# Wider passes for a mixer's natural-order projections, and attention values computed the other way round

## The chip, the cores and the metric

The kernel runs on one core of a Trainium2 chip. The time is the device time of one execution in microseconds; the kernel before takes 1060.43 us, the median of three runs (1059.81 to 1061.07). The engines of the core work side by side, each through its own list of instructions in a fixed order: TensorE (PE) multiplies matrices, VectorE (DVE) and ScalarE (ACT) do elementwise work, GpSimd (POOL) some of it and part of the DMA issues, and SyncE (SP) issues most DMAs.

## The reference

One decoder layer over 1024 tokens of width 1024. With RMS norms around each part it computes

```
p = rmsnorm(x) @ W_in      # columns split into q_a, k_a, v_a, q_r, k_r, v_r, g
a = sliding-window attention(q_a, k_a, v_a)    # 8 heads, 2 groups of keys and values, window 128, sinks
r = swish(g) * groupnorm(retention(q_r, k_r, v_r))   # 4 heads of 128, chunks of 128, rotated q and k
x = x + rmsnorm(concat(a, r) @ W_out)
u = causal conv3(rmsnorm(x) @ W_up);  x = x + rmsnorm((gelu(u_gate) * u_val) @ W_down)
```

The first projection has six groups of columns: attention queries (512), keys (128), values (128), retention queries and keys (512 each), retention values (512) and gates (512). Only the first projection, and the order of the work around it, is touched.

## The kernel before, in words

All products are in float32, made of three products of rounded halves: an operand is split into a rounded part `h` and a rest `l`, and `mm3` (lines 127 to 131) adds h\*h, h\*l and l\*h into one PSUM tile. Weights come by SP's DMA queue into a ring of three buffers (`load_w`), and are split by `split` into a ring of five pairs: the rounded part by ACT (line 119), the rest by DVE (line 120).

The 1024 tokens are worked in two halves `hh` of 512. There are two ways to project a half. `block` (line 133) makes a transposed result, 128 columns of the weight on the partitions and 512 tokens along the row: 8 steps of 3 matmuls of 512 columns into one large PSUM tile. It serves attention queries (`q_unit`, 4 blocks), keys (`k_unit`) and retention queries and keys (`rot_unit`, 8 blocks). `nat_unit` (line 262) makes a natural result, 128 tokens on the partitions and weight columns along the row: the tokens of a half are four blocks `b`, each with its own large PSUM tile, and a pass `w` covers 384 weight columns in four units `kk` of two steps each, so 24 matmuls of 384 columns per unit. Three passes cover 1152 columns: pass 0 the attention values and half of the retention values, pass 1 the other half and 128 columns of the gates, pass 2 the other 384 gate columns. After unit 3 of a pass the four tiles are emptied: attention values are scaled by the row norm and split (ACT line 282, DVE line 283), retention values copied (lines 289 and 293), gates turned into `(tanh(g r / 2) + 1) g` (ACT line 299, DVE line 300).

PSUM has four large tiles (`big`) and four small ones (`small`) in rings. A pass needs all four large ones; a `block` needs one.

What stands next to what is written out by hand. A half has a first list of units (queries, the sums for the norm `half_sums`, which have no matmul, `setup`, keys, pass 0) and a second one (8 rotation units, passes 1 and 2). `interleave` (line 504) puts steps of a second list behind each unit, spread evenly: in the first list of half 1 the retention of half 0, in the second list of each half its own attention. Attention (`att_stages`) has 8 items of scores, flip and output; the flip of an item is listed two items after its scores, the output one after the flip, 24 stages in all. Retention (`ret_stages`) has per chunk an inner step (products and transposes of the keys), an output step and a flip, 12 in all. The output step multiplies the masked inner product, which DVE writes (line 407), by the values.

A planner then fixes each engine's list from that order: it goes through the program with estimated durations and gives an engine the earliest instruction that it takes to be ready. Each engine keeps that list on the chip and waits by semaphores. The order in time of PE in the profile is the order of the program, up to one place in the later up-projection.

The functions that the change touches:

Of the kernel before, what the change touches and what calls it, by code (L numbers as in the profile page):

```python
# [8 lines left out]
F32 = mybir.dt.float32  # L9
# [5 lines left out]
P = 128  # L15
# [12 lines left out]
def tile_hymba_layer(  # L28
# [94 lines left out]
    def split_w(src, n, step, name):  # L123
        raw = load_w(src, n, name)
        return [split(raw[:, c : c + step], f"{name}_{c}", step) for c in range(0, n, step)]
# [131 lines left out]
    def turns(kk):  # L257
        if kk in (0, 3):
            return [(b, i) for b in range(4) for i in range(2)]
        return [(b, i) for i in range(2) for b in range(4)]  # L260

    def nat_unit(hh, w, kk, act, st):
        if kk == 0:
            st["pn"] = [big(f"pn{hh}_{w}_{b}") for b in range(4)]
        ops = split_w(w_inN[w, kk], 768, 384, f"n{hh}_{w}_{kk}")
        ah, al = act
        for b, i in turns(kk):
            k = 2 * kk + i
            hi, lo = ops[i]
            bs = slice(b * P, b * P + P)  # L270
            lh = ah[k // 4][:, k % 4, bs]
            ll = al[k // 4][:, k % 4, bs]
            mm3(st["pn"][b][:, :384], lh, ll, hi[:, :384], lo[:, :384], k == 0, k == 7)
        if kk < 3:
            return
        _, r, _, rhf, _, _ = st["cols"]
        for b in range(4):
            ps = st["pn"][b]
            if w == 0:
                va = m.tile([P, 2, P], F32R, tag="va", name=f"va{hh}_{b}", bufs=5)  # L280
                pv = ps[:, 0:P].rearrange("p (g d) -> p g d", g=2)
                nc.scalar.activation(va[:, :, 0:64], pv, AF.Copy, scale=r[:, b : b + 1])
                nc.vector.scalar_tensor_tensor(
                    out=va[:, :, 64:128], in0=pv, scalar=r[:, b : b + 1], in1=va[:, :, 0:64].bitcast(F32),
                    op0=ALU.mult, op1=ALU.subtract,
                )
                st["va"][4 * hh + b] = va
                vr = m.tile([P, H], F32, tag="vr", name=f"vr{hh}_{b}", bufs=4)
                nc.scalar.activation(vr[:, 0:256], ps[:, 128:384], AF.Copy)
                st["vr"][b] = vr  # L290
            else:
                if w == 1:
                    nc.scalar.activation(st["vr"][b][:, 256:512], ps[:, 0:256], AF.Copy)
                    st["gp"][b] = m.tile([P, H], F32, tag="gp", name=f"gp{hh}_{b}", bufs=4)
                src = ps[:, 256:384] if w == 1 else ps[:, 0:384]
                dst = st["gp"][b][:, 0:128] if w == 1 else st["gp"][b][:, 128:512]
                n = 128 if w == 1 else 384
                th = ttile(f"th{hh}_{w}_{b}")
                nc.scalar.activation(th[:, :n], src, AF.Tanh, scale=rhf[:, b : b + 1])
                nc.vector.scalar_tensor_tensor(  # L300
                    out=dst, in0=th[:, :n], scalar=1.0, in1=src, op0=ALU.add, op1=ALU.mult
                )

# [214 lines left out]
    for hh in range(2):  # L518
# [21 lines left out]
        first += [(q_unit, hh, 2, act, st), (half_sums, hh, st, (2, 3)), (q_unit, hh, 3, act, st), (setup,)]  # L540
        first += [(k_unit, hh, act, st)]
        first += [(nat_unit, hh, 0, kk, act, st) for kk in range(4)]
        interleave(first, prev)
        second = [(rot_unit, hh, t, h, act, st) for t in range(2) for h in range(4)]
        second += [(nat_unit, hh, w, kk, act, st) for w in (1, 2) for kk in range(4)]
        interleave(second, att_stages(hh, st), 0.95)
# [683 lines left out]
```

## Time and profile before

| | before |
|---|---|
| median of the runs | 1060.43 us (1059.81 to 1061.07) |
| profiled execution | 1060.02 us, of which the span is 1058.3 us |
| granted TensorE clock | 0.998 |
| PE busy | 1046.2 us (99%) |
| DVE busy | 819.2 us (77%) |
| ACT busy | 590.7 us (56%) |
| POOL busy | 115.9 us (11%) |
| first projection, retention and attention | from 0 to about 304 us of the span |

The times of the profile are from the first to the last instruction, so the profiled execution's own time is 1.7 us longer than its span. A row in order of time gives start, duration, engine, line, what is written and read, and, in brackets, how long the engine was idle before and who released it. Matmuls overlap: a row's duration is longer than the distance to the next row's start.

### The profile page before, as it was taken

Reading aid. Unit: us, or ns where it says so; the run is one execution under the profiler, and the core shown is the slowest. Engines: PE = TensorE matmul, PEld = TensorE weight load, DVE = VectorE, ACT = ScalarE, POOL = GpSimd, SP = SyncE. Lnnn points to the kernel's source line nnn. Section 1 sums busy time; section 2 is a strip of 40 time slices with the busy share of each in tenths; the row PEclk is TensorE's granted clock in tenths of the full one; section 3 lists DMA queues with packets and bytes.
Section 4 is the critical chain, followed back from the end, with each engine's and each line's share of the span. In section 5 each row is a group of like instructions: output and inputs, shape, how many; then the busy total and the mean of one; then the engine's idle time right before and its main releaser. Section 6 shows DMA issues by size and latency. Waiting matters only on the chain.

```text
span 1058.3 us, 14252 instructions
## 1 busy us (share of the span) xinstructions
PE 1046.2 (99%) x5000; PEld 887.3 (84%) x5000; DVE 819.2 (77%) x1409; ACT 590.7 (56%) x1138; POOL 115.9 (11%) x140
## 2 busy tenths in 40 slices
PE   9999999999999999999999999999999999999996
PEld 7988998988998888888888888888888888888885
DVE  5567777667686686987797888977878898859695
ACT  7566772466662567665555455555555546445461
POOL 1013232124322110000000000000000000000033
PEclk9999999999999999999999999999999999999999
DMA  8422543221231473854323233233233695604576
GB/s 309 133 80 61 179 174 56 94 81 61 65 107 53 166 252 116 292 212 147 139 88 121 94 116 139 95 114 119 91 139 109 240 350 167 225 35 167 179 195 116
DMA packets 54152, 150.20 MB, mean 142 GB/s; under 512 B 6464, under 2 KB 6592, under 8 KB 54080
## 3 DMA queue, kind: packets, MB, share of 16 engines
q1 hardware_dynamic: 51840, 145.09, 40.7%
q0 software_dynamic: 1952, 3.68, 2.2%
q8 instruction: 39, 0.64, 0.2%
q10 hardware_dynamic: 288, 0.52, 0.1%
q14 instruction: 33, 0.27, 0.1%
HBM read 123.57 MB, written 25.69 MB: 141 GB/s over the span
## 4 chain that ended last, share of the span: by engine, by line
issue 58%; PE 35%; ACT 2%; DVE 2%; POOL 2%; DMA 1%; SPq 0%; DVEq 0%; POOLq 0%; ACTq 0%
PE pn L128 3%; PE pn L130 3%; PE pn L129 3%; PE ps_r L128 3%; PE ps_r L129 3%; PE ps_r L130 3%; PE po L130 2%; PE po L128 2%; PE po L129 2%; DMA wr_n<-w_inN 1%; PE ps_q L129 1%; PE ps_q L130 1%; PE ps_q L128 1%; PE pS L329 1%; PE pS L328 1%
## 5 line engine op out<-in xcount | busy, mean ns | idle before, releaser
L128 PE MATMUL pd<-oh_d,sh_d 128*128 128x512 f32 x264 | 103.8, 393 | 0.0
L129 PE MATMUL pd<-ol_d,sh_d 128*128 128x512 f32 x264 | 103.2, 391 | 0.0
L130 PE MATMUL pd<-oh_d,sl_d 128*128 128x512 f32 x264 | 103.0, 390 | 0.0
L1023 POOL TENSOR_TENSOR fs<-fs,mhalf 128x1 f32<-128x1 f32 x8 | 8.8, 1105 | 593.8 <-DVE fs L1020 593.8
L720 DVE SCALAR_TENSOR_TENSOR a<-uv,cvp,a 128x1023 f32<-128x1023 f32 (+1 forms) x44 | 56.2, 1278 | 21.1 <-ACT a L717 21.1
L128 PE MATMUL pn<-oh_n,xh 128*128 128x384 f32 x192 | 65.7, 342 | 0.2 <-DVE q L235 0.2
L130 PE MATMUL pn<-oh_n,xl 128*128 128x384 f32 x192 | 64.5, 336 | 0.0
L129 PE MATMUL pn<-ol_n,xh 128*128 128x384 f32 x192 | 64.2, 335 | 0.0
L130 PEld LDWEIGHTS pd<-oh_d,sl_d 128*128 128x128 f32 x264 | 49.6, 188 | 11.3
L128 PEld LDWEIGHTS pd<-oh_d,sh_d 128*128 128x128 f32 x264 | 49.6, 188 | 10.7
L129 PEld LDWEIGHTS pd<-ol_d,sh_d 128*128 128x128 f32 x264 | 49.6, 188 | 10.5
L720 DVE SCALAR_TENSOR_TENSOR a<-ug,cvp,a 128x1023 f32<-128x1023 f32 (+1 forms) x44 | 56.2, 1278 | 1.6 <-ACT a L717 1.6
L128 PE MATMUL ps_r<-xh,oh_r 128*128 128x512 f32 x128 | 50.6, 395 | 0.0
L130 PE MATMUL ps_r<-xh,ol_r 128*128 128x512 f32 x128 | 50.0, 391 | 0.0
L129 PE MATMUL ps_r<-xl,oh_r 128*128 128x512 f32 x128 | 49.9, 390 | 0.0
L346 ACT ACTIVATE s<-s,sc,r 128x128 f32<-128x128 f32 x64 | 30.9, 483 | 30.2 <-DVE sc L340 30.2
L119 ACT ACTIVATE oh_n<-wr_n 128x384 fp32r<-128x384 f32 x48 | 24.1, 521 | 32.3 <-PE ps_q L129 8.5
L119 ACT ACTIVATE oh_o<-wr_o 128x512 fp32r<-128x512 f32 x32 | 20.0, 634 | 33.7 <-PE po L130 33.6
L728 ACT ACTIVATE sh_d<-r 128x512 fp32r<-128x512 f32 x33 | 20.8, 629 | 30.5 <-PE pd L129 23.7
L754 DVE TENSOR_TENSOR raw<-raw 128x512 f32<-128x512 f32 x22 | 15.2, 689 | 29.2 <-DMA raw<-w_u 29.1
L717 ACT ACTIVATE a<-ug,cvp 128x1024 f32<-128x1024 f32 x22 | 27.3, 1240 | 18.4 <-DVE ug L882 15.3
L128 PEld LDWEIGHTS pn<-oh_n,xh 128*128 128x128 f32 x192 | 36.1, 188 | 1.0 <-issue 0.5
(1248 smaller groups left out, 3274.4 us busy)
## 6 DMA issues: line engine op xcount, KB each, us to landing
raw<-w_u SPq DMA_DIRECT2D x44, 512.0 KB, 4.4
yd<-a SPq DMA_DIRECT2D x22, 512.0 KB, 2.9
r<-yd SPq DMA_DIRECT2D x22, 512.0 KB, 5.2
wr_n<-w_inN SPq DMA_DIRECT2D x24, 384.0 KB, 3.3
wr_r<-w_inT SPq DMA_DIRECT2D x16, 512.0 KB, 3.4
wr_o<-w_o SPq DMA_DIRECT2D x16, 512.0 KB, 3.6
wr_e<-w_u SPq DMA_DIRECT2D x11, 512.0 KB, 4.1
ud<-e SPq DMA_DIRECT2D x11, 512.0 KB, 4.5
```

What stands on the lines that cost most here:

```text
L119: in_turn("oh", nc.scalar.activation(hi[:, :n], src, AF.Copy))
L128: ins = nc.tensor.matmul(ps, lh, rh, start=first, stop=False, skip_group_check=onto)
L129: nc.tensor.matmul(ps, lh, rl, start=False, stop=False, skip_group_check=onto)
L130: nc.tensor.matmul(ps, ll, rh, start=False, stop=end, skip_group_check=onto)
L328: nc.tensor.matmul(ps[:, i, :nk], lq, kkh[:, gi, k0 : k0 + nk], start=True, stop=False)
L329: nc.tensor.matmul(ps[:, i, :nk], lq, kkl[:, gi, k0 : k0 + nk], start=False, stop=True)
L346: nc.scalar.activation(s[:, i, :], s[:, i, :], AF.Exp, scale=r8, bias=c[:, 1, i : i + 1], accum_out=c[:, 3, i : i + 1])
L717: nc.scalar.activation(a, u[:, c0 : c0 + n], AF.Identity, scale=cvp[:, b, 2:3], bias=cvp[:, b, 3:4])
L720: nc.vector.scalar_tensor_tensor(out=a[:, s:], in0=u[:, c0 + s - d : c0 + n - d], scalar=cvp[:, b, tap : tap + 1], in1=a[:, s:], op0=ALU.m ...
L728: in_turn("sh", nc.scalar.activation(hi, src, AF.Copy))
L754: nc.vector.tensor_tensor(out=a11, in0=a11, in1=a21, op=ALU.subtract)
L1023: nc.gpsimd.tensor_tensor(out=ss[:, 2:3], in0=ss[:, 3:4], in1=mhalf[:, 0:1], op=ALU.pow)
```

## The change

The weight of the natural passes is now the 1024 columns of retention values and gates, in two passes of 512 columns, so that pass 0 is all retention values and pass 1 all gates. A unit has 24 matmuls of 512 columns. The attention values leave the natural passes. A new `v_unit` makes them with `block`, transposed, as one more block of 128 weight columns; ACT copies the PSUM tile to SBUF, PE turns its four 128x128 parts back into one small PSUM tile, and ACT and DVE scale and split them as before.

The order changes with it. `v_unit` stands behind `k_unit` in the first list of both halves. In half 0 the retention values move from the end of the first list to the second, behind the 8 rotation units and ahead of the gates, so the second list still has 16 units. In half 1 they stay at the end of the first list, which has 13 units in place of 12; the second list has 12 in place of 16.

```diff
+    def v_unit(hh, act, st):
+        ps = block(w_inT[13], act, f"v{hh}")
+        vt = ttile(f"vt{hh}")
+        nc.scalar.activation(vt, ps, AF.Copy)
+        pt = small(f"pvt{hh}")
+        for b in range(4):
+            nc.tensor.transpose(pt[:, b * P : b * P + P], vt[:, b * P : b * P + P], ident)
+        r = st["cols"][1]
+        for b in range(4):
+            va = m.tile([P, 2, P], F32R, tag="va", name=f"va{hh}_{b}", bufs=5)
+            pv = pt[:, b * P : b * P + P].rearrange("p (g d) -> p g d", g=2)
+            nc.scalar.activation(va[:, :, 0:64], pv, AF.Copy, scale=r[:, b : b + 1])
+            nc.vector.scalar_tensor_tensor(
+                out=va[:, :, 64:128], in0=pv, scalar=r[:, b : b + 1], in1=va[:, :, 0:64].bitcast(F32),
+                op0=ALU.mult, op1=ALU.subtract,
+            )
+            st["va"][4 * hh + b] = va
...
-        ops = split_w(w_inN[w, kk], 768, 384, f"n{hh}_{w}_{kk}")
+        ops = split_w(w_inN[w, kk], 1024, H, f"n{hh}_{w}_{kk}")
...
-            mm3(st["pn"][b][:, :384], lh, ll, hi[:, :384], lo[:, :384], k == 0, k == 7)
+            mm3(st["pn"][b], lh, ll, hi, lo, k == 0, k == 7)
...
-                nc.scalar.activation(vr[:, 0:256], ps[:, 128:384], AF.Copy)
+                nc.scalar.activation(vr, ps, AF.Copy)
...
+                gp = m.tile([P, H], F32, tag="gp", name=f"gp{hh}_{b}", bufs=4)
+                th = ttile(f"th{hh}_{b}")
+                nc.scalar.activation(th, ps, AF.Tanh, scale=rhf[:, b : b + 1])
+                nc.vector.scalar_tensor_tensor(out=gp, in0=th, scalar=1.0, in1=ps, op0=ALU.add, op1=ALU.mult)
...
-        first += [(k_unit, hh, act, st)]
-        first += [(nat_unit, hh, 0, kk, act, st) for kk in range(4)]
+        first += [(k_unit, hh, act, st), (v_unit, hh, act, st)]
+        values = [(nat_unit, hh, 0, kk, act, st) for kk in range(4)]
+        second = [(rot_unit, hh, t, h, act, st) for t in range(2) for h in range(4)]
+        if hh == 0:
+            second += values
+        else:
+            first += values
         interleave(first, prev)
-        second = [(rot_unit, hh, t, h, act, st) for t in range(2) for h in range(4)]
-        second += [(nat_unit, hh, w, kk, act, st) for w in (1, 2) for kk in range(4)]
+        second += [(nat_unit, hh, 1, kk, act, st) for kk in range(4)]
         interleave(second, att_stages(hh, st), 0.95)
...
+    cols += list(range(640, 768))
     w_inT = blocks(w, np.array(cols))
-    ncols = np.array(list(range(640, 768)) + list(range(1792, 2816)))
-    w_inN = w[:, ncols].reshape(4, 2, P, 3, 384).transpose(3, 0, 2, 1, 4).reshape(3, 4, P, 768)
+    w_inN = w[:, 1792:2816].reshape(4, 2, P, 2, H).transpose(3, 0, 2, 1, 4).reshape(2, 4, P, 1024)
```

More of the change, by code (lines that the diff above doesn't have):

```diff
@@ L272, in nat_unit @@
             ll = al[k // 4][:, k % 4, bs]
-            mm3(st["pn"][b][:, :384], lh, ll, hi[:, :384], lo[:, :384], k == 0, k == 7)
+            mm3(st["pn"][b], lh, ll, hi, lo, k == 0, k == 7)
         if kk < 3:
             return
-        _, r, _, rhf, _, _ = st["cols"]
+        rhf = st["cols"][3]
         for b in range(4):
@@ L279, in nat_unit @@
             if w == 0:
[L280 to L287, printed above, removed]
                 vr = m.tile([P, H], F32, tag="vr", name=f"vr{hh}_{b}", bufs=4)
-                nc.scalar.activation(vr[:, 0:256], ps[:, 128:384], AF.Copy)
+                nc.scalar.activation(vr, ps, AF.Copy)
                 st["vr"][b] = vr
             else:
[L292 to L302, printed above, removed]
+                gp = m.tile([P, H], F32, tag="gp", name=f"gp{hh}_{b}", bufs=4)
+                th = ttile(f"th{hh}_{b}")
+                nc.scalar.activation(th, ps, AF.Tanh, scale=rhf[:, b : b + 1])
+                nc.vector.scalar_tensor_tensor(out=gp, in0=th, scalar=1.0, in1=ps, op0=ALU.add, op1=ALU.mult)
+                st["gp"][b] = gp
     def rot_unit(hh, t, h, act, st):
```

## The prediction

> **What bounds the kernel now.** I read the page first, then the waits of TensorE in the mixer, then a table by stage, then the order of time.
>
> ```profile
> span 1058.3 us, 14252 instructions
> PE 1046.2 (99%) x5000; PEld 887.3 (84%) x5000; DVE 819.2 (77%) x1409; ACT 590.7 (56%) x1138; POOL 115.9 (11%) x140
> ```
>
> PE is busy for all but 12 us. A busy PE is not a PE at its peak, so the next question is whether it ever waits in the stretch that the change touches. The list of PE's waits from 0 to 310 us (who waited for whom, total us, times, longest) has three rows:
>
> ```profile
> PE hot L89 <- DVE mhalf L78: 1.1, 1, 1.1
> PE ps_q L129 <- DVE xl L195: 1.0, 2, 0.7
> PE pn L128 <- DVE q L235: 0.2, 1, 0.2
> ```
>
> Two of them are the start, which the change leaves alone. So from 12 us on the mixer's time is the sum of PE's distances from one matmul's start to the next, and that is the unit in which I count. The others have room, but not much, while attention runs (stages of the second half; columns: us, then busy us of PE, PEld, DVE, ACT, POOL, clock, DMA share, GB/s):
>
> ```profile
> 208.50:261.61 53.11, 53.11 (x268) 44.85 (x266) 38.01 (x77) 35.28 (x96) 18.10 (x19) 1.00 0.22 70
> 261.61:304.43 42.82, 42.82 (x251) 41.55 (x250) 31.32 (x63) 31.25 (x82) 16.17 (x21) 1.00 0.28 87
> ```
>
> The first row is the eight rotation units, the second the eight units of passes 1 and 2; DVE is busy 72% and 73% of them, ACT 66% and 73%.
>
> **What the change takes from PE and gives to it.** The old passes are 3 passes x 2 halves x 4 blocks of rows x 8 steps x 3 products = 576 matmuls, which the groups show as three rows like this one:
>
> ```profile
> L128 PE MATMUL pn<-oh_n,xh 128*128 128x384 f32 x192 | 65.7, 342 | 0.2 <-DVE q L235 0.2
> ```
>
> The mean of 342 ns is a duration that overlaps the next one. What a matmul costs is read from PE's order of time, first and last of 45 in a row with 384 columns, and of 45 with 512:
>
> ```profile
> 44.98 0.33 PE L128 MATMUL pn<-oh_n,xh 128*128 128x384 f32 x1
> ...
> 52.61 0.33 PE L130 MATMUL pn<-oh_n,xl 128*128 128x384 f32 x1
> ```
>
> ```profile
> 19.70 0.39 PE L128 MATMUL ps_q<-xh,oh_q 128*128 128x512 f32 x1
> ...
> 29.68 0.39 PE L130 MATMUL ps_q<-xh,ol_q 128*128 128x512 f32 x1
> ```
>
> (52.61 - 44.98) / 44 = 0.1734 us and (29.68 - 19.70) / 44 = 0.2268 us. So 128 columns more cost 0.0534 us, and 3 x 0.0534 = 0.160 of the 0.1734 is columns: 0.013 us is a fixed part of each matmul. The new form has the same number of columns in all, 2 passes x 192 + 2 x 24 for the transposed values = 432 matmuls of 512 columns (432 x 512 = 576 x 384). PE's sum goes from 576 x 0.1734 = 99.9 to 432 x 0.2268 = 98.0: **-1.9 us**, the fixed part of 144 matmuls.
>
> The Trainium skill ("TensorE: Matmul & The Clock Gate", section "Back-to-back issue gap") gives N/2.4 + 2.5 ns for an isolated warm matmul of N columns. By that estimate the saving would be 144 x 2.5 ns = 0.4 us; the two pitches above show a fixed part five times larger, so I go by them.
>
> Turning the values back costs two groups of four 128x128 transposes. The trace has such a group in attention:
>
> ```profile
> 71.93 0.60 PE L361 MATMUL pT<-ident,s 128*128 128x128 f32 x4
> 72.28 0.48 PE L128 MATMUL ps_r<-xh,oh_r 128*128 128x512 f32 x1
> 72.60 0.40 PE L129 MATMUL ps_r<-xl,oh_r 128*128 128x512 f32 x1
> ```
>
> Four take 72.28 - 71.93 = 0.35 us, and the matmul after them 0.32 instead of 0.23, an entry cost of 0.09. Two groups: **+0.9 us**. The same page, section "Part 4: PE-mode transpose", speaks against the change: it gives about 275 ns for one transpose inside a kernel, so eight would be an estimated 2.2 us and the saving above would be gone. This trace shows 0.35 us for four in a row, since they overlap, and I keep that.
>
> **What it moves.** In half 0 the units of retention values go behind the eight rotation units. Before, they came straight after the key block and needed all four large PSUM buffers at once, while the last query block was not yet emptied:
>
> ```profile
> 37.28 0.34 PE L130 MATMUL pn<-oh_n,xl 128*128 128x384 f32 x1
> 37.83 0.41 PE L128 MATMUL pn<-oh_n,xh 128*128 128x384 f32 x1 [0.22 <-DVE q L235]
> 38.08 0.34 PE L129 MATMUL pn<-ol_n,xh 128*128 128x384 f32 x1
> ...
> 38.78 0.34 PE L130 MATMUL pn<-oh_n,xl 128*128 128x384 f32 x1
> 39.14 0.44 PE L128 MATMUL pn<-oh_n,xh 128*128 128x384 f32 x1
> 39.43 0.34 PE L129 MATMUL pn<-ol_n,xh 128*128 128x384 f32 x1
> ```
>
> The four distances, 0.55, 0.25, 0.36 and 0.29, are 0.76 above four pitches of 0.1734. After, one block at a time takes a buffer there, so I take **-0.8 us**. On the DMA side 24 issues of 384 KB become 16 of 512 KB plus 2 for the value block, 9.4 MB in both; SP's queue gets the rotation weights ahead of the value weights in half 0, at the same bytes per us of PE, and no wait on PE is laid to a weight load now. On ACT and DVE the splits fall from 48 to 36 on each, and the evictions of a pass become one copy, or one tanh and one product, per block; this lies beside PE and counts nothing, unless something of the next paragraph stands behind it. In half 1 rotation and gates are 12 units where rotation and two passes were 16, and attention's 24 stages are spread over them. Counting the stage lists, transposes stand directly ahead of a unit at 4 places instead of 8: **-0.4 us**.
>
> Sum without waits: -1.9 + 0.9 - 0.8 - 0.4 = -2.2 us.
>
> **Where PE could wait instead.** There are eight places where the new program order asks PE for something that was produced just before: (a) twice the transposes, which follow their own block at once, over an ACT copy; (b) in half 1 the list of 13 units pairs a half-sum unit, which has no PE work, with retention's first and second output, so these follow their inner products with no block between; (c) attention's first flip in half 1 comes after one unit, and the last three outputs come one 5.5 us unit after their flips. Each is priced as if PE simply stood, from the nearest rows.
>
> (a) In half 0 ACT copies the keys until 39.12 + 2.58 = 41.7, and the value block would end at 35.34 + 24 x 0.2268 = 40.8; a copy of 0.60 more (row of ACT L364 below) gives 42.3 and a wait of about 1.6. In half 1 ACT is freer: 0.8.
>
> ```profile
> 35.34 0.33 PE L128 MATMUL pn<-oh_n,xh 128*128 128x384 f32 x1
> ```
>
> ```profile
> 39.12 2.58 ACT L251 ACTIVATE kkh<-kn 64x512 fp32r<-64x512 f32 x4 [1.20 <-DVE kn L242]
> ```
>
> (b) The next PE work started at 154.27, the masked product was there at 155.17 + 0.75 = 155.92: 1.65 each, 3.3 for the two.
>
> ```profile
> 153.91 0.60 PE L412 MATMUL pK<-ident,rq 128*128 128x128 f32 x4
> 154.27 0.48 PE L128 MATMUL ps_q<-xh,oh_q 128*128 128x512 f32 x1
> ```
>
> ```profile
> 155.17 0.75 DVE L407 SCALAR_TENSOR_TENSOR inn<-pI,r,rm 128x512 f32<-128x512 f32 x1
> ```
>
> (c) From the end of the first scores to the normalized ones it took 222.51 + 0.69 - 215.01 = 8.2 us; the new order gives two more groups of scores, eight matmuls of 256 columns each (8 x (0.013 + 2 x 0.0534) = 0.96), and a unit of 24 x 0.2268 = 5.44, so 7.4: 0.8. From a flip to the last of its selects it took 301.31 + 0.63 - 293.74 = 8.2; the new order gives a unit, the flip itself (0.35) and an output's four matmuls (4 x 0.2268 = 0.9), so 6.7, and once 0.35 more: 4.1 together.
>
> ```profile
> 215.01 0.40 PE L128 MATMUL ps_r<-xh,oh_r 128*128 128x512 f32 x1
> ```
>
> ```profile
> 222.51 0.69 DVE L351 TENSOR_TENSOR s<-s,sc 128x512 f32<-128x512 f32 x1
> ```
>
> ```profile
> 293.74 0.60 PE L361 MATMUL pT<-ident,s 128*128 128x128 f32 x4
> ```
>
> ```profile
> 295.15 0.60 ACT L364 ACTIVATE ph<-pT 128x512 fp32r<-128x512 f32 x1
> ```
>
> ```profile
> 301.31 0.63 POOL L373 TENSOR_SCALAR_AFFINE_SELECT pl<-pl 128x512 fp32r<-128x512 f32 x1
> ```
>
> Upper end: 1.6 + 0.8 + 3.3 + 0.8 + 4.1 = 10.6 us. Lower end: nothing, because the planner may put matmuls of the next unit ahead of an instruction that it thinks not ready. The trace has one such place, in the early up-projection:
>
> ```profile
> 462.68 0.39 PE L129 MATMUL PE<-hl,oh_e 128*128 128x512 f32 x1
> 462.91 0.39 PE L128 MATMUL PE<-hh,oh_e 128*128 128x512 f32 x1
> ...
> 464.50 0.40 PE L130 MATMUL PE<-hh,ol_e 128*128 128x512 f32 x1
> ```
>
> ```profile
> 463.60 2.49 DVE L120 TENSOR_TENSOR ol_e<-wr_e,oh_e 128x512 fp32r<-128x512 f32 x4
> ```
>
> After the L129 of one block should stand its L130; eight matmuls of another block stand there instead, until the first of four DVE splits is done at about 463.60 + 0.68, and PE loses nothing. Against it stands the row at 37.83, where the order was fixed on a load that came later than planned, and PE lost 0.38. Between 0 and 10.6 I stay near the lower row: one place in three misjudged by 0.38, 8/3 x 0.38 = **+1.0 us**. Behind a waiting PE everything queues, since nothing else bounds the kernel: each us is a us of the end.
>
> The profiled execution took 1060.02 us (span 1058.3 and 1.7 around it); 1060.02 - 2.2 + 1.0 = 1058.8. The median of the runs is 1060.43, 0.4 above that execution, so the forecast for the median is **1059.2**.
>
> **Rivals.** *All gaps are filled* (chance 0.33): the eight places cost nothing, and the median is 1060.43 - 2.2 = 1058.2. For it speaks the row at 464.50, against it that the orders were fixed on times that the chip did not keep at 37.83.
>
> *PE stands in program order* (0.19), the one that ends slower: the eight places cost their price, 10.6 - 2.2 = +8.4, 1068.8 at the full price; it decides from 4.3 us of waits on, where the sum passes +2.1. For it speaks that DVE and ACT get denser in half 1: their 69.3 and 66.5 us of the two stages above, less four units' splits, come in about 84 us instead of 95.9 (33.3 us of old passes out, 21.8 of gates in), so up to 82% and 79%, and the planner's times and the chip's can part there. Against it: PE had no wait at all from 208 to 304 us.
>
> *The fixed part isn't a cost of the matmul* (0.05): if the 0.013 us belongs to something that also comes with wider ones, PE's sum stays, and 0.9 - 0.8 - 0.4 = -0.3 and the 1.0 of waits are left: 1061.1. Against it: both pitches are steady over 45 matmuls.
>
> **How the numbers follow.** A difference of 0.2% is 2.1 us, about what a measurement of this kernel can tell from no change. The forecast has 0.43. Of it and of the last rival nearly all lies within that bound; the first rival's 1058.2 is at its edge (1058.3), so I give two thirds of it and a tenth of the forecast to faster, and the slow rival beyond its point of decision to slower, all but 0.02: faster 0.27, same 0.56, slower 0.17. Range 1057.2 to 1063.0: the low end is the first rival less 1.0 (the spread of the runs, 0.6, and 0.4 for a fixed part of 0.016 in place of 0.013), the high end 1060.4 - 2.2 with 4.8 us of waits, which leaves out most of the slow rival.
>
> **What would show it.** The matmuls of the passes at 512 columns with a pitch of 0.227 and 384 of them; two groups of four transposes at 0.35 each; no wait at the first value pass of half 0; the first rotation of half 0 starting at about 41 us. In the waits of PE, a row for the transposes, for the retention output or for attention's outputs of over 1 us in total would speak for the slow rival; rows of none for the first. The output projection, which starts at 304.43 before (end of the second stage row), would start near 303.2. The prediction is wrong if the 0.227 pitch isn't kept in the new passes, or if a stage that is not named here waits.

## The result, and the profile after

The changed kernel takes 1068.1 us (median of six executions, 1066.2 to 1071.2) against 1060.1 us for the kernel before on the same chip. The ratio is 1.008, with a 95% interval of 1.007 to 1.009: slower by 0.8%, where 1059.2 us and 1057.2 to 1063.0 had been forecast. A few executions of the runs below took 1.4 to 2.6 times as long as the others and are left out; one of them is the profiled one of the run with the later transposes, which therefore has times only.

The profiled execution took 1067.9 us. From its page:

```profile
span 1066.2 us, 13905 instructions
PE 1048.1 (98%) x4864; PEld 869.2 (82%) x4864; DVE 818.4 (77%) x1389; ACT 589.5 (55%) x1112; POOL 118.1 (11%) x140
```

The span grew by 7.9 us. A table by stage tells whose. The first row of each pair runs from the first matmul of half 0's keys to the first of half 1's queries, the second from there to the output projection (us, then busy us of PE, PEld, DVE, ACT, POOL, clock, DMA share, GB/s). The kernel before:

```profile
29.91:147.57 117.66, 117.42 (x629) 106.59 (x628) 82.79 (x163) 77.02 (x194) 28.66 (x33) 1.00 0.37 115
147.57:304.43 156.86, 156.86 (x881) 142.32 (x880) 112.58 (x257) 92.22 (x224) 46.36 (x51) 1.00 0.30 90
```

The changed kernel:

```profile
29.73:151.56 121.83, 118.07 (x562) 98.52 (x561) 82.17 (x155) 75.73 (x181) 29.82 (x33) 0.99 0.34 109
151.56:312.30 160.74, 158.55 (x814) 132.84 (x813) 112.81 (x247) 92.27 (x211) 47.46 (x51) 1.00 0.30 87
```

Half 0 is 4.2 us longer and half 1 3.9 us, and PE, which was busy for all but 0.2 us of both stages, now idles 3.8 us in the first and 2.2 us in the second. The output projection starts at 312.30 instead of 304.43: the whole loss stands in front of it. The list of PE's waits of the changed kernel (who waited for whom, total us, times, longest) names where; rows with at least 0.3 us, those of the start left out:

```profile
PE pvt L268 <- ACT vt L265: 3.8, 1, 3.8
...
PE pT L365 <- DVE s L355: 0.7, 1, 0.7
PE pO L432 <- DVE inn L411: 0.6, 2, 0.4
PE pO L390 <- POOL ph L377: 0.5, 1, 0.5
...
PE pO L391 <- POOL pl L377: 0.3, 1, 0.3
```

Before there was one wait in the mixer, of 0.2 us. Now the four transposes that turn the attention values wait 3.8 us, attention's first flip 0.7, the retention outputs 0.6, and an attention output 0.8 for POOL's selects. PE's order of time at the first one:

```profile
41.52 0.39 PE L129 MATMUL ps_r<-xl,oh_r 128*128 128x512 f32 x1
45.67 1.12 PE L268 MATMUL pvt<-ident,vt 128*128 128x128 f32 x4 [3.76 <-ACT vt L265]
46.44 0.78 PE L130 MATMUL ps_r<-xh,ol_r 128*128 128x512 f32 x1
47.01 0.63 PE L128 MATMUL ps_r<-xh,oh_r 128*128 128x512 f32 x1
...
47.87 0.63 PE L130 MATMUL ps_r<-xh,ol_r 128*128 128x512 f32 x1
48.29 0.53 PE L128 MATMUL ps_r<-xh,oh_r 128*128 128x512 f32 x1
48.66 0.39 PE L129 MATMUL ps_r<-xl,oh_r 128*128 128x512 f32 x1
```

The rows show two things. The planner did put five rotation matmuls ahead of the transposes (the first row here is the last of them), but the transposes came 41.52 + 0.23 to 45.67, 3.9 us, too late, with 19 matmuls of that unit ready behind them. And the matmuls after the wait stand 0.43 us apart instead of 0.23 until 48.66: the transposes and five matmuls take 2.99 us where 0.35 + 5 x 0.227 = 1.5 us would do. So this one place costs 3.9 + 1.5 = 5.4 us. The granted clock of these 3 us is 0.51 (row in the last section). ACT's order of time says why the copy came late:

```profile
36.60 0.63 ACT L119 ACTIVATE oh_r<-wr_r 128x512 fp32r<-128x512 f32 x1 [6.07 <-DMA wr_r<-w_inT]
37.26 0.59 ACT L234 ACTIVATE q<-ps_q 64x512 fp32r<-64x512 f32 x1
37.88 1.15 ACT L119 ACTIVATE oh_r<-wr_r 128x512 fp32r<-128x512 f32 x2
40.56 2.58 ACT L251 ACTIVATE kkh<-kn 64x512 fp32r<-64x512 f32 x4 [1.53 <-DVE kn L242]
43.16 0.63 ACT L119 ACTIVATE oh_r<-wr_r 128x512 fp32r<-128x512 f32 x1
43.70 0.40 ACT L246 ACTIVATE kkh<-kkh 128x256 fp32r<-128x256 f32 x1
44.06 0.42 ACT L246 ACTIVATE kkl<-kkl 128x256 fp32r<-128x256 f32 x1
44.38 0.61 ACT L119 ACTIVATE oh_r<-wr_r 128x512 fp32r<-128x512 f32 x1
45.02 0.60 ACT L265 ACTIVATE vt<-ps_v 128x512 f32<-128x512 f32 x1
```

ACT idles 6 us for a weight load, and the splits, the query copy, the key copies and the two key halves that its list holds ahead of the value copy are all done after that. Before, the same ACT was late too, by the same kind of load:

```profile
35.82 0.53 ACT L119 ACTIVATE oh_n<-wr_n 128x384 fp32r<-128x384 f32 x1 [5.12 <-DMA wr_n<-w_inN]
```

But then the four units of pass 0 (attention values and half of the retention values), from 35.34 to 52.78, lay between the keys and the first work that needed ACT's late copies, the scores at 58.26; 0.2 us at 37.83 was all that PE waited. In the changed kernel the retention values stand behind the rotation, and the transposes ask for a copy by ACT at once.

In half 1 the waits look like this (PE in order of time; the masked inner product `inn`, the softmax `s` and the selected `ph` and `pl` come late):

```profile
174.30 0.40 PE L130 MATMUL ps_q<-xh,ol_q 128*128 128x512 f32 x1
175.09 0.46 PE L432 MATMUL pO<-vr,inn 128*128 128x128 f32 x2 [0.40 <-DVE inn L411]
...
238.81 0.28 PE L333 MATMUL pS<-kkl,q 128*128 128x256 f32 x1
239.76 0.63 PE L365 MATMUL pT<-ident,s 128*128 128x128 f32 x4 [0.67 <-DVE s L355]
...
296.85 0.50 PE L391 MATMUL pO<-cl,va 128*128 128x512 f32 x1
297.89 0.50 PE L390 MATMUL pO<-ph,va 128*128 128x512 f32 x1 [0.53 <-POOL ph L377]
```

### The profile page after: what moved, and what is told of

It reads as the page before. It is cut to its first block, busy times and chain, and to the rows that moved or that the text cites. A ratio compares the mean times of both kernels' runs of the same rounds, so it can differ in the third digit from the quotient of the medians.

```text
span 1066.2 us, 13905 instructions
## 1 busy us (share of the span) xinstructions
PE 1048.1 (98%) x4864; PEld 869.2 (82%) x4864; DVE 818.4 (77%) x1389; ACT 589.5 (55%) x1112; POOL 118.1 (11%) x140
## 4 chain that ended last, share of the span: by engine, by line
issue 58%; PE 32%; ACT 3%; DVE 2%; POOL 2%; DMA 1%; SPq 0%; DVEq 0%; POOLq 0%; ACTq 0%
PE pn L130 3%; PE pn L129 3%; PE pn L128 3%; PE ps_r L130 3%; PE ps_r L128 3%; PE ps_r L129 3%; PE po L130 2%; PE po L128 2%; PE po L129 2%; PE pO L432 1%; PE ps_q L129 1%; PE ps_q L128 1%; PE pT L365 1%; PE ps_q L130 1%; PE pO L391 1%
## 5 line engine op out<-in xcount | busy, mean ns | idle before, releaser
L128 PE MATMUL pn<-oh_n,xh 128*128 128x512 f32 x128 | 50.8, 397 | 0.0
L130 PE MATMUL pn<-oh_n,xl 128*128 128x512 f32 x128 | 50.1, 391 | 0.0
L129 PE MATMUL pn<-ol_n,xh 128*128 128x512 f32 x128 | 49.9, 390 | 0.0
L120 DVE TENSOR_TENSOR ol_r<-wr_r,oh_r 128x512 fp32r<-128x512 f32 x32 | 22.8, 722 | 20.9 <-ACT oh_r L119 18.8
L120 DVE TENSOR_TENSOR ol_o<-wr_o,oh_o 128x512 fp32r<-128x512 f32 x32 | 22.7, 718 | 17.5 <-ACT oh_o L119 17.4
```

What stands on the lines that cost most here:

```text
L120: nc.vector.tensor_tensor(out=lo[:, :n], in0=src, in1=hi[:, :n].bitcast(F32), op=ALU.subtract)
L128: ins = nc.tensor.matmul(ps, lh, rh, start=first, stop=False, skip_group_check=onto)
L129: nc.tensor.matmul(ps, lh, rl, start=False, stop=False, skip_group_check=onto)
L130: nc.tensor.matmul(ps, ll, rh, start=False, stop=end, skip_group_check=onto)
```

## The experiments

Every run changes the changed kernel, unless it says otherwise, and is compared with the kernel before on the same chip. "Start of the output projection" is that of its first matmul: 304.43 us before, 312.30 after. The diffs show the lines that matter; a comment names the half or the loop that a line stands in.

### Half 1: where retention and attention stand among the units

The first edit sets the number of retention steps behind each of the 13 units of half 1's first list by hand, so that no inner step and its output fall between the same two units. The second spreads attention's 24 stages over 16 units: the last four of the first list and the twelve of the second.

```diff
-        interleave(first, prev)
+        interleave_at(first, (prev, [1, 2, 2, 3, 3, 4, 5, 7, 8, 9, 10, 11, 12]))   # half 1
```

> The changed kernel, but in the first list of half 1 the retention steps are placed so that each output step has a query block between it and its inner step, as before the change. Theory: the waits for the masked inner product (0.6 us in the list of waits, 1.1 us in TensorE's distances) go, about 1067.0 us. Rival (this wait is paid anyway, further on): no difference from 1068.1.

```diff
-        interleave(second, att_stages(hh, st), 0.95)
+        att = [min(24, int((i + 1) * 24 / 15.2)) for i in range(15)] + [24]
+        interleave_at(first + second, (prev, ret + [12] * 12), (att_stages(hh, st), [0] * 9 + att))   # half 1
```

> The changed kernel, but in half 1 attention's 24 stages are spread over the four value units as well, 16 units in place of 12. Theory: the waits for the scores, 0.7 us, and for the selects, 0.8 us (together 2.6 us in TensorE's distances), go, about 1065.5 us. Rival: with attention beside the value units and the end of retention VectorE and ScalarE are late there, new waits of 1 to 3 us among the value units, no gain.

Without the pairs: 1067.3 us, ratio 1.0061 [1.0042, 1.0080], and the row of the retention outputs is gone from PE's waits. With attention over 16 units: 1066.4 us, ratio 1.0048 [1.0032, 1.0065], the rows of the flip and of the outputs are gone, and the output projection starts at 310.90. In the traces half 1 is 1.3 and 2.9 us shorter, where 1.1 and 2.6 were expected. Half 0, which neither edit touches, came out about 0.5 and 1.4 us longer, with waits of 4.2 and 4.4 us instead of 3.8, so less is left in the times: 0.8 us for the first, with an interval that overlaps that of the changed kernel, and 1.7 for the second.

### Half 0: what the transposes wait for

Four runs. The first lets the transposes, and the scaling behind them, follow the second rotation unit:

```diff
+            second[1] = (both, second[1], (v_turn, hh, st))   # half 0; v_turn: the transposes and what follows
```

> The changed kernel, but in half 0 the four transposes that turn the attention values back, and the scaling behind them, stand after the second rotation unit and not directly behind the value block. Theory (three separate waits of TensorE, each with a price): the 3.8 us wait for the value copy and the slow matmuls behind it (about 1.5 us) vanish, so about 1068.1 - 5.4 = 1062.7 us, the granted clock is back near 0.998, and the other waits stay. Rival (the new order is simply too dense, and a wait that is removed comes back at the next late tile): 1066 us or more, with a new wait in the rotation units of half 0.

It took 1066.7 us, ratio 1.0051 [1.0034, 1.0069]. The gain is 1.4 us and not 5.4, so the time is the rival's; where the rest went, the times alone can't say.

The second makes half 0's normalized keys without the row norm, so that nothing there waits for GpSimd's broadcast of the norms (its output leaves that factor out):

```diff
-        nc.vector.tensor_tensor(out=kn, in0=ps, in1=bs, op=ALU.mult)
+            nc.vector.tensor_scalar(out=kn, in0=ps, scalar1=1.0, scalar2=None, op0=ALU.mult)   # half 0
```

> The changed kernel, but in half 0 the keys are only copied out of PSUM and not multiplied by the broadcast row norm, so this factor is left out of half 0's keys; nothing on ScalarE waits for the broadcast then. Theory (the value copy is late because it stands behind the key copies in ScalarE's fixed list, and these wait for the norm's trip through DRAM): the value copy starts at about 41 us in place of 45.0, the wait for it falls from 3.8 us to under 1, no slow matmuls, about 1063 us. Rival (the copy is late because of the weight splits or the weight loads): the wait stays above 2.5 us and the time above 1066.

1068.2 us in a single run. The key copies moved from 40.56 to 40.24 only, the value copy from 45.02 to 44.70, and PE's wait at the transposes is 3.5 us instead of 3.8. So the norm's arrival at the keys is not by itself what makes the copy late; the rival is left, the splits that stand ahead, on a late load.

The third puts 16 products between block and transposes, of one operand pair that is ready (their result isn't used):

```diff
+            for _ in range(16):
+                nc.tensor.matmul(junk, act[0][0][:, 0, 0:P], act[0][0][:, 0, :], start=True, stop=True)
```

> The changed kernel with 16 extra matmuls of 512 columns between the value block and its transposes in half 0, whose results nobody reads; TensorE is busy for most of the wait, the wait itself ends at the same time. Theory (the slow matmuls behind the wait come from the idle time itself): the wait falls to 0.5 to 2 us, all matmuls behind it keep a distance of 0.23, the clock is near 0.998, and the time is within 1.5 us of the changed kernel although 3.6 us of work was added. Rival (they are slow because of the transposes or of a late operand): distances of 0.43 again behind the transposes, and the time 2 to 4 us longer.

1068.0 us in a single run, with 16 x 0.227 = 3.6 us more work in it. PE's row at the transposes:

```profile
45.68 0.66 PE L272 MATMUL pvt<-ident,vt 128*128 128x128 f32 x4 [1.45 <-ACT vt L265]
46.09 0.49 PE L128 MATMUL ps_r<-xh,oh_r 128*128 128x512 f32 x1
```

The transposes start at 45.68, where they started at 45.67, so they wait for a clock time and not for PE's progress; and no matmul behind them is slow (the next stands 0.41 us after four transposes). The time was free for any work that needs nothing from ACT.

The fourth puts the retention values of half 0 back into its first list, behind the attention values:

```diff
-        if hh == 0:
-            second += values
-        else:
-            first += values
+        first += values
```

> The changed kernel, but the retention values of half 0 stay at the end of the first list, as those of half 1 do; so half 0's attention too is spread over 12 units in place of 16. Theory: the value copy is as late as before, and attention's dense order costs half 0 what it costs half 1 (about 2.6 us in distances), about 1070.5 us. Rival (moving the values behind the rotation in half 0 is what costs): faster than 1068.1 by 2 us or more.

1070.4 us, ratio 1.0094 [1.0079, 1.0109], 2.4 us slower than the changed kernel, output projection at 314.77. That is what was expected. The transposes wait as before (4.2 us), since they still follow their own block. In half 0's attention, now spread over 12 units, a gate pass waits 0.6 us at 129 us for a rotated block that DVE empties late, and distances at 82 and 139 to 140 us are 0.2 to 0.4 us longer than the matmuls need. With the attention values ahead of them, the retention values did better behind the rotation, where the change put them.

### The three mends together

The later transposes and the two of half 1:

> The changed kernel with all three mends of the order: the values turned back after the second rotation unit in half 0, no output step of retention directly behind its inner step, attention of half 1 over 16 units. Theory (the matmul arithmetic of the prediction holds and the loss is these waits alone): the sum of the three, 1068.1 - 5.4 - 1.1 - 2.6 = 1059.0 us, and down to 1058.0 if the prediction's -2.2 us holds without waits; no wait of TensorE over 0.3 us after the start. Rival (the passes of 512 columns or the transposed values cost more than their matmuls): 1061 us or more with no wait to be seen.

1063.3 us, ratio 1.0026 [1.0016, 1.0036]: above the 1059.0 of the theory, and not by the rival's way, since there is a wait to be seen. Half 1 has none left, but half 0 has a new one, and slow matmuls again:

```profile
PE pS L338 <- DVE s L343: 3.1, 1, 3.1
```

```profile
58.83 0.38 PE L338 MATMUL pS<-kkh,q 128*128 128x256 f32 x1 [3.09 <-DVE s L343]
...
60.65 0.63 PE L130 MATMUL ps_r<-xh,ol_r 128*128 128x512 f32 x1
```

The scores need a PSUM tile that DVE empties (line 343), and DVE's list holds the values' scaling (line 280) ahead of that, which waits for ACT. The transposes themselves came without a wait, at 52.62, and the value copy had been there since 46.5; but ACT's list holds softmax, splits and rotation copies ahead of its part of the scaling, which starts at 56.13 only. So the wait at one place became a wait at another, by the order of ACT's and DVE's lists; whether the late load has a part in this one isn't shown. It is also the likely reason for the small gain of the later transposes alone, which no trace settles.

### Half 0 in another order

First, three rotation units in the first list, then the attention values, the transposes one unit later, and half 1 mended:

```diff
+            first += second[:3]
+            second = [(v_unit, hh, act, st), (both, second[3], (v_turn, hh, st))] + second[4:] + values   # half 0
```

> Three edits on the changed kernel. Half 0: the first three rotation units go into the first list, the attention values' block comes after them, and its four turning transposes after the next rotation unit, so that TensorE has three blocks of work while ScalarE works off its queue. Half 1: the retention output stages are spread so that no pair of them falls between the same two units, and the attention stages are spread over one unit more. Theory (all of the loss is waits at fixed places of the engines' lists, and each place can be filled by another order): no TensorE wait over 0.4 us between 35 and 65 us or at 164 to 175, 238 and 296 us, first output projection matmul at 302 to 304 us, time 1057.5 to 1059. Rival (half 0 lacks work to cover ScalarE's backlog, the wait moves on to the next stage that needs ScalarE or VectorE): a wait of 2 us or more followed by slow matmuls somewhere between 40 and 70 us, time 1061 or more.

1061.0 us, ratio 1.0002 [0.9993, 1.0011]: no different from the kernel before, and between the two expectations: just under the rival's 1061, with a shorter wait than its 2 us and no slow matmuls behind it. The wait at the transposes is gone, the output projection starts at 305.44, and one wait is left:

```profile
PE pS L338 <- DVE s L343: 1.7, 2, 1.5
```

Second, the attention values after the four units of retention values, half 1 as changed:

```diff
+            first += values + [(v_unit, hh, act, st)]   # half 0
```

> The changed kernel with half 0's retention values back in its first list, as in the kernel before, and there the attention values' block after them instead of ahead of them, so that four long units stand between the keys and the transposes. Half 1 as changed. Theory (the loss of half 0 is ScalarE's backlog at 36 to 46 us, and four units of other work hide it): no wait at the transposes beyond 1.6 us, but the denser attention of half 0 costs what it cost in the run with the values first (new waits of about 2.4 us at 82 and 128 to 140 us): 1064.5 to 1066. Rival (the transposes wait wherever they stand in half 0): 1069 or more.

1066.2 us, ratio 1.0049 [1.0035, 1.0063], which is 4.3 us below the run that differs from it only in where the attention values stand, and just above the range of the theory. There is no row for the transposes among PE's waits: four units of other work between hide ACT's lateness from them. It isn't free, for the first of these units now waits 1.1 us for a query block that DVE empties late (0.2 us in the kernel before), and the price of dense attention stays.

### The late load

The load that ACT waits for is issued at 25.1 and lands at 36.5. GpSimd stores the row norms shortly before it, each an element of 4 bytes at its own place. The next run spreads the norms by PE instead (a matmul of ones with a diagonal matrix, four per half, DVE makes the diagonals), with no such store:

```diff
-        nc.gpsimd.dma_start(rd[hh].rearrange("b p -> p b"), r)
-        nc.gpsimd.dma_start(st["bs"], rd[hh].rearrange("b p -> (b p)").partition_broadcast(P))
+            nc.vector.tensor_scalar(out=dg[:, bs], in0=ident, scalar1=r[:, b : b + 1], scalar2=None, op0=ALU.mult)
+            nc.tensor.matmul(pb[:, bs], ones, dg[:, bs], start=True, stop=True)   # for b in range(4)
+        nc.vector.tensor_copy(out=st["bs"], in_=pb)
```

> The changed kernel with the row norms spread over the partitions by four small matmuls of ones with a diagonal matrix, in place of the two GpSimd transfers through DRAM; the first of those stores single elements of 4 bytes. Theory (the store of 4-byte elements holds up the weight load that is issued at 25 us until 36.6 us, and with it ScalarE's splits and the copy of the attention values): the first rotation weights land by 30 us, ScalarE's 6 us wait ahead of their split is gone, the wait of the four turning transposes falls below 1 us and the slow matmuls behind it go: 1061.5 to 1063.5; half 1 as before. Rival (the load is late because the DMA queues are full of other loads): the load still lands after 34 us, the wait of 3 to 4 us stays, 1067 to 1069.

1066.1 us, ratio 1.0049 [1.0035, 1.0063]. ACT in order of time:

```profile
30.44 0.62 ACT L119 ACTIVATE oh_r<-wr_r 128x512 fp32r<-128x512 f32 x1
...
42.16 0.60 ACT L270 ACTIVATE vt<-ps_v 128x512 f32<-128x512 f32 x1
```

The first rotation weight is split at 30.44 instead of 36.60, the value copy comes at 42.16 instead of 45.02, the wait of the transposes is gone, and no matmul near them is slow. The scores of half 0 start at 47.67 where they started at 51.86. So the mechanism was right. The time was not: 2.0 us gained and not 5.4. Half 0 ends 4.2 us earlier (147.36 instead of 151.56), with 0.8 us of spreading matmuls in it. Half 1 is 2.4 us longer, mostly because the spreading there waits 1.0 us for DVE's diagonals and takes 1.0 us more, all on PE's path.

Together with half 1's order:

> The same spreading of the norms by TensorE, and beside it half 1 with the retention output stages and the attention stages spread as in the first run of this group; the attention values are turned directly behind their block in both halves. Theory (the 4-byte store and the places in half 1 are all of the loss): no TensorE wait over 1 us between 35 and 340 us, first output projection matmul at 302 to 304 us, 1057 to 1059.5. Rival (half 0's waits stay or move to the scores): 1061 to 1064.

1061.8 us, ratio 1.0011 [1.0002, 1.0020], output projection at 306.80. The spreading's waits (1.3 us) are the only ones left in the mixer, and they and its matmuls hold it above the range. The time is in the rival's range, but half 0's waits neither stayed nor moved to the scores.

A cheaper way to leave out the 4-byte store: in half 0 one transpose on PE and a store of four rows of 512 bytes.

```diff
+            nc.tensor.transpose(pr[0:4, 0:P], r, ident)
+            nc.vector.tensor_copy(out=rt, in_=pr[0:4, 0:P])
+            nc.gpsimd.dma_start(rd[hh], rt)   # half 0
```

> The changed kernel, and half 0's row norms are turned by one TensorE transpose, so that GpSimd's transfer stores four rows of 512 bytes instead of 512 single elements; half 1 untouched. Theory (the single-element store keeps back the weight load, and the change took away the work that hid this): the first rotation weights' load lands by 30 us, the four turning transposes wait under 0.5 us, first output projection matmul 4.5 to 5.5 us earlier than in the changed kernel (312.30), at 306.8 to 307.8, time 1062.5 to 1063.6. Rival (a norm transfer through DRAM holds the queues whatever its form): load after 34 us, time 1067 to 1068.5.

Ratio 1.0063 [1.0050, 1.0077], times of 1065.9 to 1068.9 us, 1066.5 in the profiled execution, with the output projection at 311.30: far less gain than expected. The DMA issues between 20 and 40 us (median us from issue to landing at the end), first of the changed kernel:

```profile
wr_r<-w_inT SPq DMA_DIRECT2D x4, 512.0 KB, 9.7
...
rd<-r_pre POOLq DMA_DIRECT2D x1, 2.0 KB, 10.1
```

and of this run:

```profile
wr_r<-w_inT SPq DMA_DIRECT2D x4, 512.0 KB, 3.3
...
rd<-rt POOLq DMA_DIRECT2D x1, 2.0 KB, 3.7
```

The store holds back the other loads, as the theory has it. Of the changed kernel's four loads, the three issued between 25 and 30 us, while the store was under way, took 9.2 to 11.4 us. In this run the store moved to 30.82, so the first load, issued at 25.25, has no store beside it and takes 3.2 us; but the third, issued at 31.12, has the dense store beside it, and takes 3.2 us too. So it is the form of the store that counts and not only its time. But ACT is late for another reason now:

```profile
39.29 2.58 ACT L258 ACTIVATE kkh<-kn 64x512 fp32r<-64x512 f32 x4 [3.16 <-DVE kn L249]
...
43.75 0.60 ACT L272 ACTIVATE vt<-ps_v 128x512 f32<-128x512 f32 x1
```

The norms' transpose stands behind the last query block on PE, so that GpSimd issues its store at 30.82 instead of 22.92; the keys wait for the norms, the key copies for the keys, and the value copy, some splits and key halves behind them, comes 1.3 us earlier only. The transposes wait 2.2 us, and slow matmuls follow.

The same with half 1's order, and the control, the kernel before with the same store:

> The changed kernel with half 0's norms stored in rows of 512 bytes and half 1's retention output and attention stages spread, the values turned directly behind their block in both halves. Theory (the two edits add up, since they remove waits at different places): no TensorE wait over 0.6 us between 35 and 340 us, first output projection matmul at 302 to 303.5 us, time 1057.5 to 1059, below the kernel before. Rival (each mend uncovers the next backlog, as the score wait did in the run of both orders): 1060 to 1062.

> The kernel before with half 0's norms stored in rows of 512 bytes, as a control. Theory (in the kernel before the four value units hide the late load, all but the two waits of 0.3 and 0.1 us at 37 to 39 us and a slow pass or two): 1059 to 1060, a gain of at most 1 us. Rival (the store costs the kernel before as much as the changed one, so that it isn't the change that uncovers it): 1057 or less.

With half 1's order: 1063.0 us, ratio 1.0020 [1.0011, 1.0029], above both expectations, with a wait of 2.5 us at the transposes and no other in the mixer. The control: 1059.3 us, ratio 0.9985 [0.9976, 0.9993], output projection at 303.57. By the times the store of single elements costs the kernel before 1.4 us (0.7 to 2.5 by the interval); its trace shows 0.4 us in the stage of half 0, and 0.5 of the earlier output projection lies ahead of the store. Either way the kernel stays above the 1057 that the rival asked for: the late load was there, and the units that the change moved hid nearly all of it.

### Without waits

The last two take the dense store and half 1's order, and in half 0 either the transposes behind the first rotation unit, or the order with three rotation units first.

```diff
+            second[0] = (both, second[0], (v_turn, hh, st))   # half 0
```

> The run with the dense store and half 1's order, and in half 0 the four turning transposes stand after the first rotation unit instead of behind the block. The trace of that run has one TensorE wait left (2.7 us ahead of the transposes), and between the first query block and the output projection it is otherwise without waits. Theory (this wait is free time that another order fills): no TensorE wait over 0.6 us between 35 and 340 us, first output projection matmul at 302.5 to 303.5 us, time 1058 to 1059.5, about that of the kernel before with the dense store (1059.29). Rival (the scores wait in place of the transposes, as in the run of all three orders): a wait over 1.5 us between 46 and 60 us, 1061 or more.

> The run with half 0 reordered (three rotation units ahead of the attention values) and the dense store of the norms. Its one wait over 0.6 us, 1.9 us at 66 us, stands behind VectorE, which eviction by eviction is late since the store. Theory (this lateness is the store's): the wait falls below 0.8 us, first output projection matmul at 302.5 to 304 us, 1058 to 1059.5. Rival (VectorE's own order sets it): the wait stays between 1.5 and 2.5 us, 1060 to 1061.5.

The first, as expected: 1058.5 us (1058.1 to 1059.7), ratio 0.9980 [0.9971, 0.9988], the output projection at 303.08. All of PE's waits from start to end:

```profile
PE hot L89 <- DVE mhalf L78: 1.1, 1, 1.1
PE ps_q L129 <- DVE xl L195: 0.7, 1, 0.7
PE pR L493 <- POOL gnt L486: 0.2, 1, 0.2
```

The second: 1061.0 us, ratio 1.0001 [0.9992, 1.0010]; its wait of 1.7 us at the scores is unchanged, so that one is DVE's own order and not the store's.

The first is the version that shows what the change is worth. Its two stages, and those of the control (the kernel before with the same store) below:

```profile
29.93:146.53 116.60, 116.60 (x562) 97.53 (x561) 83.27 (x156) 75.61 (x181) 30.72 (x34) 1.00 0.33 111
146.53:303.08 156.55, 156.55 (x814) 133.01 (x812) 111.64 (x247) 92.18 (x211) 46.36 (x51) 1.00 0.32 90
```

```profile
29.43:146.72 117.29, 117.29 (x631) 106.74 (x630) 83.68 (x164) 76.47 (x194) 29.17 (x34) 1.00 0.34 113
146.72:303.57 156.85, 156.85 (x881) 142.32 (x880) 112.62 (x257) 92.17 (x223) 46.46 (x51) 1.00 0.30 90
```

Neither has a gap. Against the control the change shortens half 0 by 0.7 us and half 1 by 0.3. Against the changed kernel half 0 is 121.83 - 116.60 = 5.2 us shorter and half 1 160.74 - 156.55 = 4.2, together 9.4 us: the price of the waits and of the slow matmuls behind them. This version is faster than both kernels; against the control its 1058.5 stands beside 1059.3, with intervals that overlap, so the change's own worth, 1.0 us by the traces, isn't shown in the times.

## Why the prediction was wrong

**The matmul arithmetic held.** The new passes run at a pitch of 0.227 us and are 384 in number. Summed by kind between the two waitless kernels above, the distances of all projection matmuls fall from 223.4 to 221.2 us, -2.2, where the prediction had -1.9 for the fixed part, -0.4 for fewer entries and +0.2 for the entries behind the new transposes. The entries were wrong in kind: projection matmuls that directly follow other work, which pay the entry, are 40 where they were 41. The eight transposes take 0.85 us together, where 0.7 was forecast. The scores take 0.4 us more, which the prediction had not. That makes -0.9 of the -1.0 in the stages.

**The -0.8 for the four PSUM buffers** was half right. The gaps at 37 to 39 us are gone, but they did not all belong to the buffers: with the dense store, the kernel before loses 0.4 us of its first stage, and the wait there, with no change of units.

**The step that failed is the +1.0 us of waits**: "Between 0 and 10.6 I stay near the lower row: one place in three misjudged by 0.38". It should have been 9.4 us. Taken by place:

| place | price if PE stands | measured |
|---|---|---|
| (a) transposes, half 0 | 1.6 | 5.4 (3.9 late, 1.5 of slow matmuls) |
| (a) transposes, half 1 | 0.8 | none |
| (b) retention outputs, twice | 3.3 | 1.1 (distances of 0.61, 0.37 and 0.79 us against 0.23) |
| (c) first flip | 0.8 | 0.8 (0.95 against 0.12) |
| (c) last outputs | 4.1 | 1.8 (0.51, 1.04, 0.34, 0.70 and 0.34 against 0.23) |

The measured column sums to 9.1 of the 9.4 (5.4 for 5.2 in half 0, 3.7 for 4.2 in half 1). So the planner fills gaps in part, as the row at 464.50 had suggested, with six matmuls at each place of (b) and five at the transposes; but the lateness on the chip was longer than what it filled, and half 0's place was priced at less than a third. That price (1.5 by the prediction's own figures, 42.3 - 40.8) took ACT's list of the kernel before and put one copy behind it, from 41.7 to 42.3. The copy ran from 45.02: the keys were copied 1.4 us later, and two splits and two key halves, 1.9 us, stood between. The price did not ask what ACT's list would hold ahead of that copy once the rotation weights' splits come first, nor what ACT itself was waiting for. And it had no term for what comes behind a wait, 1.5 us of matmuls at half the clock. The row was there to read: ACT idled 5.12 us for a weight load at 35.82 in the kernel before. The prediction said that no wait on PE is laid to a weight load, which was so, and passed over that a wait on ACT was, under the cover of the units that it then moved away.

**The rival "PE stands in program order"** was priced at 1068.8, and 1068.1 was measured, but the places don't share out as it had them: of half 0's 5.4 us its price held 1.6, and its reason, that ACT and DVE become denser in half 1, can bear on 4.2 of the 9.4 us only. That the sums agree is luck. The rival with all gaps filled, 1058.2, is close to the version without waits (1058.5), but that took three further edits, and the dense store among them makes the kernel before faster too: without waits the change is worth 1.0 us by the traces, not 2.2.

**What would show it.** The output projection was to start near 303.2. It started at 312.30, and in the version without waits at 303.08. The other signs held: 384 matmuls at 0.23 us, no wait at the first value pass of half 0, the first rotation there at 40.62 us; and the waits stood at the places that (a) to (c) name. The rows for the transposes, over 1 us, spoke for the slow rival, as the prediction said that they would.

## What to carry to other kernels

When an edit moves work away from in front of something, ask what that work was hiding, and look for it among the idle times of the engines that were *not* the bound: a 5 us wait of a half-idle engine costs nothing until the bottleneck's next instruction needs its output. An engine's list is fixed here, so the new 0.6 us copy cost what stood ahead of it in ACT's list on the chip, not its own duration. And mending one such wait can bring another where the moved work now stands in the way, as the transposes behind the second rotation unit did at the scores; look at the next place too, take away the lateness, or keep enough work between.

## What the runs showed of the hardware

**A store of single elements slows other loads.** 2 KB stored as 512 elements of 4 bytes took 10.1 us to land, and three 512 KB loads on another queue took 9.2 to 11.4 us beside it; the same 2 KB in four rows took 3.7 us, with loads of 3.2 and 3.3 beside it. It is so in half 1 of the changed kernel as well: the store issued at 162.71 took 9.5 us, and the load issued at 163.46 took 12.5. The Trainium skill ("DMA: Bandwidth & Descriptors", section "Queues, rings and completion order") says that a DMA engine takes turns between queues packet by packet and drains a whole packet first. That a transfer on one queue holds up another fits engines that take turns; the runs show neither the packets' turns nor why the single elements take so long.

**TensorE's clock can halve after a wait, and the wait's length alone doesn't decide it.** Stages behind the transposes of half 0 (clock is the third figure from the end), of the changed kernel after 3.8 us of idle time:

```profile
45.67:48.67 3.00, 3.00 (x10) 2.58 (x11) 0.75 (x3) 0.73 (x2) 0.00 (x0) 0.51 0.51 175
```

of the run with the dense store after 2.2 us:

```profile
44.40:48.40 4.00, 4.00 (x13) 3.22 (x14) 0.94 (x4) 1.58 (x4) 0.00 (x0) 0.58 0.40 131
```

and of the run with the dense store and half 1's order after 2.5 us:

```profile
44.80:48.80 4.00, 3.98 (x20) 3.37 (x21) 1.72 (x5) 1.87 (x5) 0.00 (x0) 1.00 0.38 131
```

The granted clock is 0.51 and 0.58 in the first two and 1.00 in the third, after a longer wait than the second's; after 1.45 us (the run with 16 products) no slow matmul was seen. The Trainium skill ("TensorE: Matmul & The Clock Gate", section "Part 1: The HAM clock gate") has the clock halved after an idle window of about 3.4 us, with windows that run freely. The halving agrees (0.43 us against 0.227 us a matmul), and windows that run freely would allow two answers to equal waits; but here it happened after 2.2 us, shorter than the window that it states. What decides it stays open.
